# First block without GpSimd arithmetic: lower halves and three projection products moved to VectorE

## The chip, the cores and the metric

The program runs on one core of a Trainium2 chip, in one launch. The metric is the device time of one execution in microseconds (us), as the median of several runs. The engines of the core are TensorE (PE in the profile, with PEld for its weight loads), VectorE (DVE), ScalarE (ACT), GpSimd (POOL), and SyncE (SP), which here issues nearly all transfers. Each engine takes its own instructions in a fixed order and waits in that order for data of the others.

## The reference, cut to what matters

A sequence of 256 rows of 1024 numbers goes through a first block (an mLSTM group and a differential attention side by side, then a mixture of 32 experts) and through two layers of a second block, which this change does not touch. All arithmetic is float32. The part in question is the head of the first block:

```
h = rmsnorm(x, norm1_g)                    # 256 x 1024
proj = h @ w_in                            # 1024 x 3072, six parts of 512 columns
c, vm, z, qd, kd, vd = split(proj, 6)
y_m = mlstm_group(c, vm, z, ...)           # conv, gates, 4 heads, sigmoid(z) * h
y_d = diff_attention(qd, kd, vd, ...)      # 4 heads, each two softmaxes
x = x + concat(y_m, y_d) @ w_out
x = x + hier_moe(rmsnorm(x, norm2_g), ...) # router, 32 experts of 1024 x 512
```

## The kernel before, in words

A float32 product is made of three products of reduced-precision operands. Every operand is split into an upper half, which ScalarE writes by a cast (`whi` for weights, line 169; `xTh` for the input, line 388), and a lower half, which is the operand minus its upper half (`wlo`, line 173; `xTl`, line 389). TensorE then adds hi times hi, hi times lo and lo times hi into one PSUM tile.

The six parts of the projection run one after another, in the order c, vm, qd, kd, z, vd. The first five are `dense_T` (line 218): the result stands transposed, 4 x 128 columns by 256 rows, in two PSUM tiles `ps[0]` and `ps[1]`. Each takes eight blocks of 128 of the 1024 input columns, two blocks (one `split`, 128 x 1024 numbers) at a time, with 24 matmuls of 128x256 per split and 96 per part. There are four buffers for each kind of half, so a split waits until TensorE is done with the split four before it.

The input is not divided by the rows' norm before the products. The norm's factor `rn` (one number per row) is worked out by VectorE beside the first part (lines 395, 262 to 277, 397), spread over all partitions by two small TensorE products (line 425) into `R` (line 426), and every part's result is multiplied by `R` on its way out of PSUM: `cpad` (431), `vT` (436), `qd` (443 and 444), `kd` (457 and 458), `zs` (604 and 605).

GpSimd takes a share of this. It subtracts the lower halves of two of the four splits of part c and of all four of part vm (`pool=` in lines 420 and 433), the lower halves of the second half of the input (`NP = (1,)`, line 389), and the products with `R` for qd, kd and z, for which ScalarE first copies the PSUM tile to SBUF:

```
nc.scalar.copy(qd[:, 2 * c:2 * c + 2, :], ps[c])
nc.gpsimd.tensor_mul(qd[:, 2 * c:2 * c + 2, :], qd[:, 2 * c:2 * c + 2, :], R)
```

For a split whose lower half comes from GpSimd, `dense_T` puts the matmuls on `wlo` behind all matmuls on `whi` of that split (the `order.sort` of line 231).

The order of each engine's instructions is not the order of the code: a scheduler places them from their dependencies and priorities. `high_priority` pulls a piece ahead (the splits, and all of the mLSTM group under `early()`), and `issue_after` holds one back: the products of line 425 are tied behind the 81st matmul of part c (`r_behind = 80`). The mLSTM group (conv `cy`, `cth`, `ca`; gates `gt` to `um`; decay matrices `W` and `WS`; `HN`; `ym`) and the four attention heads (line 647 to 665) are thus placed among the matmuls of the parts qd to vd. Weights are loaded 1 MB at a time into four buffers, by SP; the experts' weights follow in the same queue (line 940) into rings that use memory the first block gives up.

The names in the rows: `raw` a loaded weight, `nh` the input times the norm's weight, `um` and `uT` the gates and their transpose, `BM` the table of relative biases (loaded by line 450 from `bigd`, which GpSimd's queue writes from `tb`), `mx` and `tp` small PSUM tiles, `acc` the large ones, `idle` a dummy operand.

Of the kernel before, what the change touches and what calls it, by code (L numbers as in the profile page):

```python
# [92 lines left out]
class K:  # L93
# [121 lines left out]
                    self.mm3(ps[t][:, :n], xh[:, kx + k, ts], xl[:, kx + k, ts], hi[:, k % 2, :n], lo[:, k % 2, :n],  # L215
                             first and k == 0, last and k == nk - 1)

    def dense_T(self, xT, kx, raw, nk, ps, hold={}, pool=()):

        xh, xl = xT
        mm = self.nc.tensor.matmul
        for k in range(0, nk, 2):
            with ExitStack() as es:
                for ins in hold.get(k, ()):
                    es.enter_context(self.tc.issue_after(ins.ins))
                hi, lo = self.split(raw, k, 2, 512, k in pool)
            order = [(j, c, i) for j in range(2) for c in range(4) for i in range(3)]
            if k in pool:  # L230
                order.sort(key=lambda z: z[2] == 2)
            for j, c, i in order:
                w, x = ((hi, xh), (hi, xl), (lo, xh))[i]
                first = k + j == 0 and i == 0
                ins = mm(ps[c // 2][:, c % 2, :], w[:, j, c * P:(c + 1) * P], x[:, kx + k + j, :],  # L235
                         start=first and c % 2 == 0, stop=k + j == nk - 1 and i == 2, skip_group_check=True)
                self.mms.append(ins)
                if first and c % 2 == 0:
                    head = ins
                elif first:  # L240
                    self.tc.add_manual_dep(ins.ins, head.ins.name, mybir.DependencyInfo(
                        mybir.DependencyClass.NoSync, mybir.DependencyReason.DATA))
# [76 lines left out]
    def first_mixers(self, x, outer):  # L319
        nc, tc, A = self.nc, self.tc, self.A  # L320
        with ExitStack() as es:
# [5 lines left out]
            hT = self.hT = self.xT_tile(8, self.yp, "xT")  # L327
            half = lambda: pz.tile([P, 512], F32, name="nh", bufs=4)
            w_in = A["w_in"][0]
            wc = []  # L330
            for n in range(2):
                raw = self.wp.tile([P, 4, 512], F32, name="raw")
# [15 lines left out]
            wv = self.load(w_in[:, 512:1024], D, 512)  # L348
# [20 lines left out]
            hold = {}  # L369
            with early():  # L370

                ps = self.tp.tile([P, 4, P], F32, name="tp")
# [3 lines left out]
            for n in range(2):  # L376
                for t in range(NT):
                  with tc.high_priority(offset=3000 if n == 0 else 900):
                    ps = self.tp.tile([P, 4, P], F32, name="tp")
                    for i in range(4):  # L380
                        cs = slice(n * 512 + i * P, n * 512 + (i + 1) * P)
                        nc.tensor.transpose(ps[:, i, :], x[:, t, cs], self.ident)
                    h = half().rearrange("p (i q) -> p i q", i=4)
                    with tc.issue_after(hold[2][1].ins) if n else ExitStack():
                        nc.vector.tensor_tensor(h, ps, gc[:, 4 * n:4 * n + 4].unsqueeze(2).to_broadcast([P, 4, P]),
                                                op=ALU.mult)
                    hi, lo = (z[:, 4 * n:4 * n + 4, t * P:(t + 1) * P] for z in hT)
                    hold[4 * n + 2 * t] = (nc.scalar.copy(hi, h),
                                           (nc.gpsimd if n in self.NP else nc.vector).tensor_sub(lo, h, hi))  # L389
            hold = {2: hold[2], 4: hold[6], 6: hold[6]}  # L390
            ss = pz.tile([P, NT, 2], F32, name="nss")
            for t in range(NT):
# [24 lines left out]

            ps = self.accT()
            self.mms = []
            self.dense_T(hT, 0, wc, 8, ps, hold, (0, 2))  # L420
            R = p.tile([P, S], F32, name="R")
            pr = self.tp.tile([P, 4, P], F32, name="tp")
            with early(), tc.issue_after(self.mms[self.r_behind].ins):
# [3 lines left out]
            R = R.unsqueeze(1).to_broadcast([P, 2, S])  # L427
# [2 lines left out]
            for c in range(2):  # L430
                nc.vector.tensor_mul(cpad[:, 2 * c:2 * c + 2, 3:], ps[c], R)
            ps = self.accT()
            self.dense_T(hT, 0, wv, 8, ps, pool=(0, 2, 4, 6))
            vT = pz.tile([P, 4, S], F32, name="vT")
            for c in range(2):
                nc.vector.tensor_mul(vT[:, 2 * c:2 * c + 2, :], ps[c], R)
# [2 lines left out]
            ps = self.accT()  # L439
            self.dense_T(hT, 0, self.load(w_in[:, 1536:2048], D, 512), 8, ps)  # L440
            qd = p.tile([P, 4, S], F32, name="qd", tag="qd", bufs=1)
            for c in range(2):
                nc.scalar.copy(qd[:, 2 * c:2 * c + 2, :], ps[c])
                nc.gpsimd.tensor_mul(qd[:, 2 * c:2 * c + 2, :], qd[:, 2 * c:2 * c + 2, :], R)
            self.mms = []
            ps = self.accT()
            self.dense_T(hT, 0, self.load(w_in[:, 2048:2560], D, 512), 8, ps)
# [6 lines left out]
                                 self.c("zc")[:, P:].unsqueeze(1).to_broadcast([P, 4, P]))  # L454
            kd = p.tile([P, 4, S], F32, name="kd", tag="kd", bufs=1)
            for c in range(2):
                nc.scalar.copy(kd[:, 2 * c:2 * c + 2, :], ps[c])
                nc.gpsimd.tensor_mul(kd[:, 2 * c:2 * c + 2, :], kd[:, 2 * c:2 * c + 2, :], R)
            with early():
                ca = pz.tile([P, 4, S], F32, name="ca")  # L460
                for c in range(4):
# [83 lines left out]
                for t in range(NT):  # L545
# [3 lines left out]
                    for h2 in range(2):  # L549
                        pn = self.mx.tile([P, 2, P + 1], F32, name="mx")  # L550
                        num.append(pn)
                        for j in range(2):
                            h = 2 * h2 + j
# [46 lines left out]
            ps = self.accT()  # L600
            self.dense_T(hT, 0, self.load(w_in[:, 1024:1536], D, 512), 8, ps)
            zs = p.tile([P, 4, S], F32, name="zs")
            for c in range(2):
                nc.scalar.copy(zs[:, 2 * c:2 * c + 2, :], ps[c])
                nc.gpsimd.tensor_mul(zs[:, 2 * c:2 * c + 2, :], zs[:, 2 * c:2 * c + 2, :], R)
                nc.scalar.activation(zs[:, 2 * c:2 * c + 2, :], zs[:, 2 * c:2 * c + 2, :], AF.Tanh, scale=0.5)
            nc.vector.tensor_scalar(zs, zs, 0.5, 0.5, op0=ALU.mult, op1=ALU.add)
            vd = p.tile([P, NT, 512], F32, name="vd")
# [3 lines left out]
            ps = self.accs(2, side)  # L612
# [704 lines left out]
            (nc.vector.tensor_copy if c % 2 else nc.scalar.copy)(dst[c], ps[c])  # L1317

    ahead = 1000
    NP = (1,)  # L1320

    EH = (0, 0, 0, 2)
    r_behind = 80
# [8 lines left out]
    hold = ()  # L1332
# [768 lines left out]
```

## Time and profile before

| what | value |
|---|---|
| median of 3 runs | 1774.81 us (1773.97 to 1777.96) |
| the profiled execution's own time | 1774.42 us |
| its span in the profile | 1772.70 us, mean TensorE clock 0.988 of full |
| TensorE busy | 1717.6 us (97%) |
| VectorE busy | 976.3 us (55%) |
| ScalarE busy | 740.3 us (42%) |
| GpSimd busy | 99.3 us (6%) |

Busy time of TensorE is modelled: a matmul counts until its result is out, and matmuls overlap, so 97% does not say that the engine did all it could. A row of the timeline gives start, duration, engine, line, operation, output and inputs; in brackets stands the idle time of the engine just before, and what ended it. Times run from the span's start. The first block up to the experts takes the first 172 us or so; the experts follow until about 610 us.

### The profile page before, as it was taken

Reading aid. Unit: us, or ns where it says so; the run is one execution under the profiler, and the core shown is the slowest. Engines: PE = TensorE matmul, PEld = TensorE weight load, DVE = VectorE, ACT = ScalarE, POOL = GpSimd, SP = SyncE. Lnnn points to the kernel's source line nnn. Section 1 sums busy time; section 2 is a strip of 40 time slices with the busy share of each in tenths; the row PEclk is TensorE's granted clock in tenths of the full one; section 3 lists DMA queues with packets and bytes.
Section 4 is the critical chain, followed back from the end, with each engine's and each line's share of the span. In section 5 each row is a group of like instructions: output and inputs, shape, how many; then the busy total and the mean of one; then the engine's idle time right before and its main releaser. Section 6 shows DMA issues by size and latency. Waiting matters only on the chain. (4 is left out here: it accounts for less than half of the span.)

```text
span 1772.7 us, 27358 instructions
## 1 busy us (share of the span) xinstructions
PE 1717.6 (97%) x11007; PEld 1315.3 (74%) x11007; DVE 976.3 (55%) x1868; ACT 740.3 (42%) x1260; POOL 99.3 (6%) x153
## 2 busy tenths in 40 slices
PE   7999999999999999999989999999999998999998
PEld 6876443444334379799878999987889987999997
DVE  6686122222222277764675765557766467575555
ACT  3463111111011146564644454444566464455443
POOL 4010000000000020000011000002000002000000
PEclk8999999999999999999999999999999999999999
DMA  8457999999999974256445755554335644455552
GB/s 266 147 210 298 413 420 420 420 418 420 420 420 419 413 235 136 69 179 199 148 144 160 237 188 187 187 176 157 112 93 179 202 143 131 167 173 186 188 190 83
DMA packets 153465, 414.51 MB, mean 234 GB/s; under 512 B 13347, under 2 KB 42868, under 8 KB 128632
## 3 DMA queue, kind: packets, MB, share of 16 engines
q1 hardware_dynamic: 152408, 410.49, 64.5%
q0 software_dynamic: 784, 2.18, 0.4%
q8 instruction: 87, 1.43, 0.3%
q14 instruction: 42, 0.34, 0.1%
q10 hardware_dynamic: 144, 0.07, 0.0%
HBM read 411.63 MB, written 2.12 MB: 233 GB/s over the span
## 5 line engine op out<-in xcount | busy, mean ns | idle before, releaser
L173 DVE TENSOR_TENSOR wlo<-raw,whi 128x1024 fp32r<-128x1024 f32 (+3 forms) x376 | 445.7, 1187 | 297.9 <-ACT whi L169 297.3
L169 ACT CAST whi<-raw 128x1024 fp32r<-128x1024 f32 (+4 forms) x384 | 385.2, 1005 | 396.3 <-PE acc L235 161.2
L235 PE MATMUL acc<-xTh,whi 128*128 128x256 f32 x992 | 286.5, 290 | 0.0
L235 PE MATMUL acc<-xTl,whi 128*128 128x256 f32 x992 | 284.2, 288 | 1.0 <-DVE xTl L389 1.0
L235 PE MATMUL acc<-xTh,wlo 128*128 128x256 f32 x992 | 279.6, 289 | 0.0
L1084 PE MATMUL acc<-raw,XT 128*64 128x512 f32 x1024 | 243.0, 603 | 3.8 <-DMA raw<-in_w_eg 2.7
L235 PEld LDWEIGHTS acc<-xTl,whi 128*128 128x128 f32 x992 | 192.6, 194 | 5.3 <-issue 3.5
L235 PEld LDWEIGHTS acc<-xTh,whi 128*128 128x128 f32 x992 | 192.6, 194 | 3.4 <-issue 2.4
L235 PEld LDWEIGHTS acc<-xTh,wlo 128*128 128x128 f32 x992 | 188.7, 193 | 5.6 <-issue 5.0
L1084 PEld LDWEIGHTS acc<-raw,XT 128*64 128x64 f32 x1024 | 74.6, 137 | 129.1 <-issue 115.4
L181 PE MATMUL acc<-wlo,xTh 128*128 128x512 f32 (+4 forms) x368 | 129.4, 352 | 1.7 <-DVE wlo L173 1.7
L182 PE MATMUL acc<-whi,xTl 128*128 128x512 f32 (+4 forms) x368 | 129.0, 351 | 0.2
L180 PE MATMUL acc<-whi,xTh 128*128 128x512 f32 (+4 forms) x368 | 128.5, 349 | 0.0
L1107 PE MATMUL acc<-raw,hidT 128*64 128x512 f32 x512 | 119.2, 597 | 4.4 <-DMA raw<-in_w_ed 4.2
L180 PE MATMUL acc<-whi,ffh 128*128 128x512 f32 x256 | 100.9, 394 | 0.0
L182 PE MATMUL acc<-whi,ffl 128*128 128x512 f32 x256 | 100.4, 392 | 0.0
L181 PE MATMUL acc<-wlo,ffh 128*128 128x512 f32 x256 | 100.4, 392 | 0.0
L1107 PEld LDWEIGHTS acc<-raw,hidT 128*64 128x64 f32 x512 | 35.6, 137 | 71.7 <-issue 61.4
L1049 DVE SCALAR_TENSOR_TENSOR yl<-acc,gs,yh 128x512 fp32r<-128x512 f32 x32 | 24.0, 751 | 107.0 <-ACT yh L1048 107.0
L1048 ACT ACTIVATE yh<-acc,gs 128x512 fp32r<-128x512 f32 x32 | 22.0, 687 | 140.0 <-PE acc L1107 140.0
L181 PEld LDWEIGHTS acc<-wlo,xTh 128*128 128x128 f32 x368 | 69.2, 188 | 10.6 <-DVE wlo L173 2.8
L182 PEld LDWEIGHTS acc<-whi,xTl 128*128 128x128 f32 x368 | 69.2, 188 | 7.8 <-DVE xTl L302 1.5
(690 smaller groups left out, 3061.4 us busy)
## 6 DMA issues: line engine op xcount, KB each, us to landing
raw<-in_w_in SPq DMA_DIRECT2D x70, 1024.0 KB, 5.1
raw<-in_w_eg SPq DMA_DIRECT2D x64, 1024.0 KB, 19.9
raw<-in_w_eu SPq DMA_DIRECT2D x64, 1024.0 KB, 19.9
raw<-in_w_ed SPq DMA_DIRECT2D x64, 1024.0 KB, 19.9
raw<-in_w_ff SPq DMA_DIRECT2D x64, 1024.0 KB, 5.2
raw<-in_w_out SPq DMA_DIRECT2D x12, 1024.0 KB
raw<-in_w_branch SPq DMA_DIRECT2D x12, 1024.0 KB, 5.4
raw<-in_w_in SPq DMA_DIRECT2D x8, 792.0 KB, 4.7
```

The lines of the kernel that those rows point to most:

```text
L169: nc.scalar.copy(hi[:, :nk, :n], src)
L173: ins = (nc.gpsimd if pool else nc.vector).tensor_sub(lo[:, :nk, :n], src, hi[:, :nk, :n])
L180: mm(ps, ahi, bhi, start=start, stop=False)
L181: mm(ps, ahi, blo, start=False, stop=False)
L182: self.mm_ins = mm(ps, alo, bhi, start=False, stop=stop)
L235: ins = mm(ps[c // 2][:, c % 2, :], w[:, j, c * P:(c + 1) * P], x[:, kx + k + j, :], start=first and c % 2 == 0, stop=k + j == nk - 1 and ...
L1048: nc.scalar.activation(yh[:rows], py[n][:rows], AF.Copy, scale=gs)
L1049: nc.vector.scalar_tensor_tensor(yl[:rows], py[n][:rows], gs, yh[:rows].bitcast(F32), op0=ALU.mult, op1=ALU.subtract)
L1084: nc.tensor.matmul(ps[64 * z:64 * z + 64], XT[:, k, 64 * (o + z):64 * (o + z + 1)], ww[z][k], start=k == 0, stop=k == 7)
L1107: nc.tensor.matmul(py[n][64 * z:64 * z + 64], hT[:, k, 64 * z:64 * z + 64], ww[z][k][:, n * 512:(n + 1) * 512], start=k == 0, stop=k == 3)
```

## The change

All lower halves of `dense_T` and of the input are subtracted by VectorE, the special order of matmuls for GpSimd's splits goes, and the products with `R` for qd, kd and z are done by VectorE straight from PSUM, without ScalarE's copy.

```diff
-    def dense_T(self, xT, kx, raw, nk, ps, hold={}, pool=()):
+    def dense_T(self, xT, kx, raw, nk, ps, hold={}):
...
-                hi, lo = self.split(raw, k, 2, 512, k in pool)
-            order = [(j, c, i) for j in range(2) for c in range(4) for i in range(3)]
-            if k in pool:
-                order.sort(key=lambda z: z[2] == 2)
-            for j, c, i in order:
+                hi, lo = self.split(raw, k, 2, 512)
+            for j, c, i in [(j, c, i) for j in range(2) for c in range(4) for i in range(3)]:
...
-                                           (nc.gpsimd if n in self.NP else nc.vector).tensor_sub(lo, h, hi))
+                                           nc.vector.tensor_sub(lo, h, hi))
...
-            self.dense_T(hT, 0, wc, 8, ps, hold, (0, 2))
+            self.dense_T(hT, 0, wc, 8, ps, hold)
...
-            self.dense_T(hT, 0, wv, 8, ps, pool=(0, 2, 4, 6))
+            self.dense_T(hT, 0, wv, 8, ps)
...
-                nc.scalar.copy(qd[:, 2 * c:2 * c + 2, :], ps[c])
-                nc.gpsimd.tensor_mul(qd[:, 2 * c:2 * c + 2, :], qd[:, 2 * c:2 * c + 2, :], R)
+                nc.vector.tensor_mul(qd[:, 2 * c:2 * c + 2, :], ps[c], R)
...
-                nc.scalar.copy(kd[:, 2 * c:2 * c + 2, :], ps[c])
-                nc.gpsimd.tensor_mul(kd[:, 2 * c:2 * c + 2, :], kd[:, 2 * c:2 * c + 2, :], R)
+                nc.vector.tensor_mul(kd[:, 2 * c:2 * c + 2, :], ps[c], R)
...
-                nc.scalar.copy(zs[:, 2 * c:2 * c + 2, :], ps[c])
-                nc.gpsimd.tensor_mul(zs[:, 2 * c:2 * c + 2, :], zs[:, 2 * c:2 * c + 2, :], R)
+                nc.vector.tensor_mul(zs[:, 2 * c:2 * c + 2, :], ps[c], R)
```

The scheduler places the whole first block anew. Line numbers of the changed kernel are smaller by 3 in the first lines, by 5 or so behind the products. VectorE from the first input tile to the norm, before:

```order
L385 TENSOR_TENSOR nh<-tp,gc 128x512 x2
L389 TENSOR_TENSOR xTl<-nh,xTh 128x4x128 x2
L385 TENSOR_TENSOR nh<-tp,gc 128x512 x2
L173 TENSOR_TENSOR wlo<-raw,whi 128x1024 x2
L401 COPY vec<-tp 128x32
L598 TENSOR_SCALAR dg<-vec 128x1
L395 TENSOR_TENSOR nss<-nss 128x2
L262 TENSOR_SCALAR rs_v<-nss,eps 128x2
```

VectorE at the same place in the changed kernel:

```order
L382 TENSOR_TENSOR nh<-tp,gc 128x512 x2
L173 TENSOR_TENSOR wlo<-raw,whi 128x1024
L386 TENSOR_TENSOR xTl<-nh,xTh 128x4x128 x2
L173 TENSOR_TENSOR wlo<-raw,whi 128x1024
L382 TENSOR_TENSOR nh<-tp,gc 128x512 x2
L386 TENSOR_TENSOR xTl<-nh,xTh 128x4x128 x2
L173 TENSOR_TENSOR wlo<-raw,whi 128x1024 x2
L398 COPY vec<-tp 128x32
L593 TENSOR_SCALAR dg<-vec 128x1
L392 TENSOR_TENSOR nss<-nss 128x2
L259 TENSOR_SCALAR rs_v<-nss,eps 128x2
```

Four instructions more stand ahead of the norm (two `wlo`, two `xTl`); two further `wlo` stand inside the norm's chain and two behind it, ahead of `R`. TensorE around the two products that spread the norm, before (`acc_229` and `acc_230` belong to part c, `acc_352` and `acc_353` to part vm):

```order
L235 MATMUL acc_230<-xTh,whi 128x256
L235 MATMUL acc_230<-xTl,whi 128x256
L235 MATMUL acc_230<-xTh,wlo 128x256
L425 MATMUL tp<-const,rn 128x128 x2
L235 MATMUL acc_230<-xTh,whi 128x256
L235 MATMUL acc_230<-xTl,whi 128x256
L235 MATMUL acc_230<-xTh,wlo 128x256
```

TensorE there in the changed kernel:

```order
L232 MATMUL acc_230<-xTh,wlo 128x256
L232 MATMUL acc_352<-xTh,whi 128x256
L232 MATMUL acc_352<-xTl,whi 128x256
L232 MATMUL acc_352<-xTh,wlo 128x256
L232 MATMUL acc_352<-xTh,whi 128x256
L422 MATMUL tp<-const,rn 128x128 x2
L232 MATMUL acc_352<-xTl,whi 128x256
L232 MATMUL acc_352<-xTh,wlo 128x256
```

The products on `rn` stood behind 81 matmuls of the projections and stand behind 100 now, four into part vm. VectorE around the gates, where qd ends, before:

```order
L516 TENSOR_SCALAR NM<-Mx 4x256
L453 TENSOR_TENSOR BM<-BM,const 128x4x128
L517 TENSOR_TENSOR um<-NM,bb 4x256
L173 TENSOR_TENSOR wlo<-raw,whi 128x1024
L523 COPY uT<-mx 128x72
L536 SCALAR_TENSOR_TENSOR W<-mx,uT,const_132 128x256
```

VectorE at that place in the changed kernel (`acc_487` and `acc_488` hold part qd):

```order
L511 TENSOR_SCALAR NM<-Mx 4x256
L440 TENSOR_TENSOR qd<-acc_487,R 128x512
L512 TENSOR_TENSOR um<-NM,bb 4x256
L440 TENSOR_TENSOR qd<-acc_488,R 128x512
L173 TENSOR_TENSOR wlo<-raw,whi 128x1024
L449 TENSOR_TENSOR BM<-BM,const 128x4x128
L518 COPY uT<-mx 128x72
L531 SCALAR_TENSOR_TENSOR W<-mx,uT,const_132 128x256
```

The two products for qd come in, one ahead of `um` and one behind it, and `BM` moves from ahead of `um` to behind the `wlo`. On TensorE four matmuls of part kd now stand between the first `NM` product (line 531) and the first product on `qk` (line 533). The products for kd stand in VectorE's queue inside the second norm of the mLSTM group, those for z inside its third; the attention heads are interleaved with that group in another order. In SP's queue the only move is the fourth load of `w_out`, which stood behind the first two expert loads and now stands ahead of them. GpSimd keeps its memsets and its two transfers for the bias table. Behind the first block the order is unchanged on every engine, but for a GpSimd set-up instruction that stands at that engine's first arithmetic.

## Rows read from the trace of the kernel before

**Rows 1.** Stretches: busy time of each engine, TensorE clock, DMA share, GB/s.

```profile
50.00:89.00 39.00, 37.13 (x262) 32.24 (x262) 29.00 (x58) 17.76 (x25) 3.30 (x2) 0.91 0.45 145
89.00:127.00 38.00, 35.17 (x224) 28.98 (x224) 33.54 (x114) 25.71 (x64) 5.73 (x4) 1.00 0.50 184
...
172.60:177.60 5.00, 4.95 (x24) 2.13 (x26) 0.76 (x2) 0.10 (x1) 0.00 (x0) 1.00 0.20 39
177.60:600.00 422.40, 415.21 (x1964) 172.26 (x1962) 104.31 (x190) 58.87 (x110) 0.00 (x0) 0.99 1.01 419
```

**Rows 2.** TensorE's waits, 0 to 200 us: total, times, longest.

```profile
PE tp L425 <- DVE rn L397: 4.5, 1, 4.5
...
PE mx L478 <- DVE tb L409: 1.5, 1, 1.5
...
PE mx L533 <- DVE uT L523: 1.4, 1, 1.4
...
PE mx L675 <- ACT vd L615: 1.1, 1, 1.1
PE acc L235 <- DVE xTl L389: 1.0, 1, 1.0
...
PE acc L641 <- POOL kd L458: 0.7, 1, 0.7
```

**Rows 3.** Timeline of GpSimd, from 8 us: start, duration, instruction, wait before.

```profile
8.27 2.36 POOL L173 TENSOR_TENSOR wlo<-raw,whi 128x1024 fp32r<-128x1024 f32 x1 [5.44 <-ACT whi L169]
...
18.40 7.25 POOL L173 TENSOR_TENSOR wlo<-raw,whi 128x1024 fp32r<-128x1024 f32 x3 [0.32 <-ACT whi L169]
...
65.66 3.30 POOL L444 TENSOR_TENSOR qd<-qd,R 128x512 f32<-128x512 f32 x2 [18.81 <-ACT qd L443]
```

**Rows 4.** Timeline of VectorE in the same stretches.

```profile
8.74 3.05 DVE L389 TENSOR_TENSOR xTl<-nh,xTh 128x512 fp32r<-128x512 f32 x2 [1.32 <-ACT xTh L388]
...
19.35 1.52 DVE L395 TENSOR_TENSOR nss<-nss 128x2 f32<-128x2 f32 x1
20.90 2.34 DVE L262 TENSOR_SCALAR rs_v<-nss,eps 128x2 f32<-128x2 f32 x1
...
23.48 2.19 DVE L267 TENSOR_SCALAR rs_i<-rs_i 128x2 int32<-128x2 int32 x1
...
65.72 0.67 DVE L453 TENSOR_TENSOR BM<-BM,const 128x512 f32<-128x512 f32 x1
66.43 1.40 DVE L517 TENSOR_TENSOR um<-NM,bb 4x256 f32<-4x256 f32 x1
67.86 2.18 DVE L173 TENSOR_TENSOR wlo<-raw,whi 128x1024 fp32r<-128x1024 f32 x1
```

**Rows 5.** VectorE by line and shape, 0 to 130 us: busy, mean ns.

```profile
L431 DVE TENSOR_TENSOR cpad<-acc,R 128x512 f32<-128x512 f32 x2 | 1.4, 692 | 2.1 <-PE acc L235 2.1
...
L276 DVE SCALAR_TENSOR_TENSOR rs_q<-rs_q,rs_v 128x2 f32<-128x2 f32 x3 | 0.5, 161 | 0.1
```

**Rows 6.** The page's costliest group: busy, mean ns.

```profile
L173 DVE TENSOR_TENSOR wlo<-raw,whi 128x1024 fp32r<-128x1024 f32 (+3 forms) x376 | 445.7, 1187 | 297.9 <-ACT whi L169 297.3
```

**Rows 7.** TensorE at the wait for the norm.

```profile
27.78 0.55 PE L425 MATMUL tp<-const,rn 128*128 128x128 f32 x1 [4.46 <-DVE rn L397]
```

**Rows 8.** Stretches at full and at half clock, columns as in rows 1.

```profile
18.00:20.00 2.00, 2.00 (x19) 2.00 (x18) 1.50 (x4) 1.37 (x2) 1.68 (x2) 1.00 1.06 413
28.40:32.40 4.00, 4.00 (x21) 4.00 (x21) 1.31 (x3) 0.41 (x1) 0.00 (x0) 0.50 0.27 32
70.40:76.80 6.40, 6.40 (x21) 4.94 (x21) 3.32 (x7) 2.02 (x4) 0.00 (x0) 0.50 0.50 164
```

**Rows 9.** SP's queue: start, duration, issue.

```profile
31.54 4.38 SPq L159 DMA_DIRECT2D raw<-in_w_in  x4
53.48 3.67 SPq L450 DMA_DIRECT2D BM<-bigd  x8
```

**Rows 10.** DMA issues of the bias table: KB each, median us to landing.

```profile
BM<-bigd SPq DMA_DIRECT2D x8, 64.0 KB, 2.2
```

More of the change, by code (lines that the diff above doesn't have):

```diff
@@ L1319 @@
     ahead = 1000
-    NP = (1,)
     EH = (0, 0, 0, 2)
```

## The prediction

> **What bounds the kernel now.** I read the table of stretches first. From 177.6 us to 600 us the experts take their weights as fast as the DMA engines move them: share 1.01, 419 GB/s [rows 1]. So there TensorE, though modelled as busy, is fed by the transfers. Just ahead of it, from 172.6 to 177.6 us, the DMA share is only 0.20 at 39 GB/s [rows 1]: the rings are full, and transfers go on only when the first experts free their buffers. The time at which the first block ends therefore starts everything after it, and since the order behind the block does not change, a microsecond gained in the first block should be a microsecond of the whole. That is the first step of the forecast.
>
> Second, the waits of TensorE up to 200 us: one of 4.5 us for `rn`, and then 1.5 (`tb`), 1.4 (`uT`), 1.1 (`vd`), 1.0 (`xTl`) and 0.7 (`kd`) [rows 2]. [...]
>
> Fourth, why `rn` and `uT` are late. GpSimd's three subtractions run from 18.40 for 7.25 us, to 25.65 [rows 3], about 2.4 us each. Beside them VectorE's tiny operations on 128x2 numbers take 1.52, 2.34 and 2.19 us and end at 20.87, 23.24 and 25.67 [rows 4], at the ends of GpSimd's instructions. An operation of that size takes 161 ns when nothing runs beside it [rows 5]. So VectorE stands still while GpSimd subtracts. The same shows beside GpSimd's two products (65.66 us, 3.30 us [rows 3]): `um` of 4x256 takes 1.40 us and the `wlo` behind it 2.18 us [rows 4] against a mean of 1.187 [rows 6].
>
> **The change part by part.** The sum is made against the profiled execution's own 1774.42 us (1.72 of it outside the span), which is 0.39 under the median of 1774.81.
>
> *VectorE's load.* It gains six `wlo`: 6 x 1.187 = 7.1 us [rows 6]. It gains two `xTl`: the pair at 8.74 took 3.05 beside GpSimd [rows 4]; alone I take the 0.69 us of a 128x512 operation [rows 5] for each, 1.4 together. And it gains six products with `R` from PSUM, of the same shape and source as `cpad`: 6 x 0.692 = 4.2 us [rows 5]. Together +12.7 us. It loses the stretches. Of the rows shown: 3.05 - 1.4, 1.52 + 2.34 + 2.19 - 3 x 0.16, 1.40 - 0.4 (my estimate for 4x256, from `BM`'s 0.67 for 512 numbers per partition [rows 4]) and 2.18 - 1.19, in sum 9.2 us, and these are only part of the places where GpSimd works. So VectorE's load hardly rises, and it falls where TensorE waits for it. GpSimd's arithmetic and six copies of ScalarE go; nobody waits for what they leave free.
>
> *Term A, up to 50 us.* In the new order TensorE meets the norm's products behind 100 matmuls instead of 81. It came there at 27.78 - 4.46 = 23.3 us [rows 7]; 19 matmuls at 19 in 2.0 us [rows 8] add 2.0, and the wait of 1.0 for `xTl` ahead of it [rows 2] falls away: 24.3. On VectorE the chain from 19.35 us to the products at 27.78 [rows 4, 7] lasted 8.4 us, 5.6 of it stretch; alone 2.8, and with the two `wlo` put inside it 5.2. What comes ahead of the chain is two `wlo` and two `xTl` more (3.8) and a stretch of 1.7 less at 8.74; at least 1.3 of the difference fits into VectorE's idle time there (1.32 in one row alone [rows 4]), so the chain starts about where it did and `rn` is ready near 24.6. Left of the wait: 0.3. If the cover failed and all 2.1 came on top, the wait would be 2.4. With the wait gone the clock should stay up: the 21 matmuls from 28.4 to 32.4 took 4.0 us and take 21 x 2.0 / 19 = 2.2 at full clock [rows 8], 1.8 back. The waits for `xTl` (1.0) and `tb` (1.5), both VectorE's work beside GpSimd [rows 2], go with the stretch. A = 4.5 - 0.3 + 1.8 + 1.0 + 1.5 = 8.5 us less. Bounds: 2.1 if only the difference at the norm is gained and the clock falls all the same (4.5 - 2.4), 9.0 at most.
>
> *Term B, 50 to 89 us.* VectorE is busy 29.00 of 39 us here [rows 1]. On the way to `uT` the stretch of `um` (1.0) and of the `wlo` behind it (1.0) go, `BM` (0.67) moves from ahead of `um` to behind it and stays on the way, and the two products for qd (1.4) come in. VectorE is thus 0.6 us earlier, and four matmuls of part kd now stand on TensorE ahead of the product that waits, 4 x 2.0 / 19 = 0.4 [rows 8]. Of the 1.4 I leave 0.6, and count 0.8. The half clock from 70.4 to 76.8 us gives back up to 3.2 of its 6.4 us [rows 8] if it does not fall. I take all 3.2, since the idle time ahead is less than half of what it was and has matmuls of 128x256 inside it; B = 4.0 less. Bounds: 4.6 less (the wait gone as well), or 0.5 more if `uT` gets later by half the added products.
>
> GpSimd's queue also writes the bias table that `BM` needs. SP's loads of it are issued from 53.48 for 3.67 us [rows 9] and land 2.2 us later [rows 10], at 59.35, and VectorE takes it at 65.72 [rows 4], 6.4 us of slack. The table starts from VectorE's `tb`, so most of its transfer moves along when VectorE gets earlier; were it to stay at its old time while VectorE's `BM` came 8.5 us earlier, less the 3.0 us of `um`, qd and `wlo` put ahead of it (0.4 + 1.4 + 1.2), 0.9 us of slack would be left.
>
> *Term C, 89 to 127 us.* VectorE is busy 33.54 of 38 us [rows 1]. It gains four products, 2.8 us [rows 5], and loses the stretch beside GpSimd's 5.73 busy us [rows 1], at most 5.7 and by the share of the 65.66 place (2.0 of 3.30) some 3. TensorE's waits for `vd` and `kd`, 1.1 + 0.7 [rows 2], are for ScalarE and GpSimd, whose part in them shrinks. I count 1.0 less. Bounds: 1.8 less, or 2.8 more if all four products stand on the path. *The fourth load of w_out*, put ahead of two expert loads, delays those by 1 MB, some 2.5 us at 419 GB/s [rows 1]; the nearly idle DMA of 172.6 to 177.6 hides it.
>
> Sum: 8.5 + 4.0 + 1.0 = 13.5 less, 1760.9 us for an execution like the profiled one, and with its 0.39 a median of 1761.3 us.
>
> **The rivals.** *The clock falls anyway and VectorE binds behind kd.* For it: 0.6 us of the wait for `uT` is still there, and VectorE is already busy 88% from 89 to 127 [rows 1]. Then B brings nothing and C turns from 1.0 less to 2.5 more: 1761.3 + 4.0 + 3.5 = 1768.8. Against it: the load hardly rises.
>
> *The bias table comes late.* The row above shows slack of 6.4 us shrinking, to 0.9 at the worst. If the table lands 2 us behind VectorE's want of it, VectorE stands ahead of `uT`, term B goes (4.0) and 2.0 come on top: 1767.3. No row shows that transfer delayed. [...]
>
> *No change.* If the experts' start hung on a transfer of fixed time, the block's gain would be given back and the time stay at 1774.8. The share of 0.20 from 172.6 to 177.6 [rows 1] speaks against it.
>
> *Slower.* The PSUM tiles of kd and z were freed by ScalarE (busy 25.71 of 38), and are now freed by VectorE (33.54 of 38) [rows 1], which takes them only when its queue of gates and heads comes to them. If TensorE waited at each of these four tiles as long as it did for the norm, 4.5 us [rows 2], that is +18 and 1779.3. It decides from 3.4 us a tile on (13.5 / 4). Against it: TensorE had only 1.8 us of waits there, and VectorE has 4.5 us of room.
>
> **How the numbers follow.** The forecast 0.62, with its own range of 1757 to 1766 (term A's clock, B's clock, C's bounds); the fallen clock 0.19; the late table 0.04; no change 0.06; slower 0.09. The 8-in-10 range goes from 1756 to 1770.5 and takes in the first two rivals. A measurement of this kernel tells about 0.2% (3.5 us) from no change. Faster by more: 0.62 + 0.19 + 0.04 = 0.85, and 0.01 for a weaker form of "no change"; within: 0.05; slower: 0.09.
>
> **What would show it.** No operation of 128x2 on VectorE over 0.3 us up to 30 us; no wait over 1 us at the norm's products, and TensorE's clock at 1.00 from 28 to 34 us; part vm ending 8 to 9 us earlier; `uT` waited for by under 0.8 us and no stretch at 0.50 behind it; from 80 us on the same work 12 to 13 us earlier, and no wait for VectorE over 1 us at kd, z and the heads; the first expert's start and the end of the span earlier by the same amount. The forecast is wrong if TensorE stands at a PSUM tile that VectorE has not yet multiplied, if a half clock appears at another place, or if the first block's gain is not found at 600 us.

## The result: 1757.3 us, and the profile after

The changed kernel took 1757.3 us (median of 5 runs, 1755.61 to 1757.93), the kernel before, in the same job, 1777.96. The ratio is 0.9885, 95% interval 0.987 to 0.99. In the profiled executions the span fell from 1772.70 to 1756.1 us, by 16.6. The forecast was 1761.3: faster by somewhat more than forecast. How much the change saves is known less well than that it saves: between medians taken together it is 20.7 us here, 19.7 and 15.9 on two other chips (1776.04 and 1756.3, 1775.23 and 1759.36), and the profiled execution of before (1774.42) is one of its faster ones.

Of TensorE's waits up to 200 us that [rows 2] shows, one is left; the list (total, times, longest) now begins with the load of the input; waits of the router follow, which stood there before as well:

```profile
PE tp L379 <- DMA x<-in_x: 3.4, 1, 3.4
...
PE acc L232 <- DVE xTl L386: 0.2, 1, 0.2
```

VectorE beside the norm and beside `uT`, the counterpart of [rows 4]:

```profile
15.23 1.29 DVE L386 TENSOR_TENSOR xTl<-nh,xTh 128x512 fp32r<-128x512 f32 x2
...
19.57 0.16 DVE L392 TENSOR_TENSOR nss<-nss 128x2 f32<-128x2 f32 x1
19.77 0.23 DVE L259 TENSOR_SCALAR rs_v<-nss,eps 128x2 f32<-128x2 f32 x1
...
20.24 0.17 DVE L264 TENSOR_SCALAR rs_i<-rs_i 128x2 int32<-128x2 int32 x1
...
24.36 0.17 DVE L394 COPY rn<-rs_i 128x2 f32<-128x2 f32 x1
...
57.94 0.42 DVE L512 TENSOR_TENSOR um<-NM,bb 4x256 f32<-4x256 f32 x1
58.38 0.69 DVE L440 TENSOR_TENSOR qd<-acc,R 128x512 f32<-128x512 f32 x1
58.99 1.22 DVE L173 TENSOR_TENSOR wlo<-raw,whi 128x1024 fp32r<-128x1024 f32 x1
60.13 0.68 DVE L449 TENSOR_TENSOR BM<-BM,const 128x512 f32<-128x512 f32 x1
```

The 128x2 operations that took 1.52, 2.34 and 2.19 us take 0.16, 0.23 and 0.17; the pair of `xTl` 1.29 instead of 3.05; `um` 0.42 instead of 1.40. TensorE meets its two former waits without one (no bracket behind the row):

```profile
25.78 0.60 PE L422 MATMUL tp<-const,rn 128*128 128x128 f32 x4
...
61.01 0.70 PE L528 MATMUL mx<-qk 128*128 128x256 f32 x2
```

The stretches of [rows 1, 8] (columns as there), the last two shifted by the 16.2 us that the experts now start earlier:

```profile
28.40:32.40 4.00, 4.00 (x36) 4.00 (x35) 4.00 (x11) 0.40 (x2) 0.00 (x0) 1.00 0.49 50
50.00:89.00 39.00, 38.98 (x277) 33.74 (x276) 32.46 (x107) 17.72 (x39) 0.00 (x0) 1.00 0.53 176
70.40:76.80 6.40, 6.40 (x51) 6.01 (x50) 5.96 (x23) 1.68 (x2) 0.00 (x0) 1.00 0.50 166
89.00:127.00 38.00, 37.88 (x220) 32.36 (x218) 31.53 (x83) 25.68 (x58) 0.00 (x0) 1.00 0.66 250
156.40:161.40 5.00, 5.00 (x24) 2.05 (x26) 0.76 (x2) 0.01 (x1) 0.00 (x0) 1.00 0.15 29
161.40:600.00 438.60, 431.14 (x2031) 178.09 (x2027) 107.13 (x195) 60.97 (x114) 0.00 (x0) 0.99 1.01 419
```

Both half clocks of [rows 8] are gone, TensorE is nearly without a gap from 50 to 127 us (38.98 of 39.00 and 37.88 of 38.00), and the experts run at 419 GB/s as before, from an earlier start.

To place the gain I cut the first block at six events of the timeline: the first projection product, the end of the last `vT`, the first product on `uT` (line 528), the first product with `V` and `WS`, the first with `vd` and `aT`, and the end of the last sum into `x` after `w_out`. The lengths in us, with those of all experiments:

| kernel | to `vT` | to `uT` | to `V,WS` | to `vd,aT` | to `x` | sum |
|---|---|---|---|---|---|---|
| before | 40.94 | 19.21 | 11.61 | 43.42 | 31.53 | 146.7 |
| after | 31.18 | 18.51 | 8.75 | 39.17 | 31.55 | 129.2 |
| after_again | 31.55 | 18.50 | 8.75 | 39.17 | 31.54 | 129.5 |
| after_third | 31.35 | 18.51 | 8.76 | 39.16 | 31.53 | 129.3 |
| gp_reads_norm | 38.36 | 18.50 | 8.77 | 39.21 | 31.55 | 136.4 |
| gp_writes_norm | 32.99 | 18.50 | 8.76 | 39.22 | 31.51 | 131.0 |
| gp_reads_ut | 30.93 | 19.98 | 11.78 | 39.20 | 31.56 | 133.5 |
| products_only | 43.67 | 18.48 | 8.75 | 39.20 | 31.53 | 141.6 |
| halves_only | 30.99 | 19.27 | 10.07 | 43.44 | 31.53 | 135.3 |
| kd_z_back | 31.43 | 18.52 | 8.76 | 41.66 | 31.46 | 131.8 |
| copy_kept | 30.30 | 18.52 | 8.40 | 39.90 | 35.57 | 132.7 |

after_again and after_third are the changed kernel once more, on the chips of other experiments. Its three executions agree within 0.02 us in all stages but the first, which spreads by 0.37. Over all ten executions here that have the changed kernel's order up to `vT` and nothing added, the first stage takes 30.1 to 31.6 us. Whole times scatter by several us, mostly behind the first block (the three spans are 1756.1, 1758.0 and 1754.9 us, their sums here 129.2 to 129.5), so the stages tell more than the medians.

A stage does not always hold the same work. The third and the fourth, before and then after:

```profile
70.24:81.85 11.61, 11.61 (x51) 9.25 (x51) 5.87 (x12) 3.23 (x6) 0.00 (x0) 0.71 0.28 90
81.85:125.27 43.42, 40.59 (x270) 34.24 (x268) 38.91 (x138) 28.06 (x63) 5.73 (x4) 1.00 0.46 163
```

```profile
61.01:69.76 8.75, 8.75 (x53) 7.16 (x54) 5.78 (x13) 3.77 (x7) 0.00 (x0) 1.00 0.74 274
69.76:108.93 39.17, 39.17 (x264) 33.73 (x262) 36.74 (x141) 24.54 (x59) 0.00 (x0) 1.00 0.46 162
```

Six matmuls of 128x256 that stood in the fourth stage now stand in the second (four) and the third (two). TensorE's busy time in the fourth falls by 1.4 us for that, and its idle time from 2.8 us to nothing.

### The profile page after: what moved, and what is told of

It reads as the page before. It is cut to its first block, busy times and chain, and to the rows that moved or that the text cites. A ratio compares the mean times of both kernels' runs of the same rounds, so it can differ in the third digit from the quotient of the medians.

```text
span 1756.1 us, 27356 instructions
## 1 busy us (share of the span) xinstructions
PE 1710.9 (97%) x11007; PEld 1310.5 (75%) x11007; DVE 971.2 (55%) x1882; ACT 737.0 (42%) x1254; POOL 72.2 (4%) x139
## 5 line engine op out<-in xcount | busy, mean ns | idle before, releaser
L232 PE MATMUL acc<-xTh,wlo 128*128 128x256 f32 x992 | 285.0, 287 | 0.0
```

## Experiments

The theory: GpSimd instructions that read SBUF hold VectorE up; the gain is the sum of what that cost in each stage, with the clock that falls behind TensorE's waits. The rival: the gain comes from other queues and another order of matmuls, and the long VectorE rows cost nothing.

**GpSimd's reading brought back, for nobody.** The order of the other engines stays word for word.

```diff
+            dum = pz.tile([P, 4, S], F32, name="dum", tag="ca", bufs=1)
+            with tc.high_priority(offset=3000), tc.issue_after(hold[6][1].ins):
+                for _ in range(3):
+                    nc.gpsimd.tensor_sub(dum, hT[1][:, 4:8, :], hT[0][:, 4:8, :])
```

> The changed kernel, and three more subtractions of 128x1024 on GpSimd, of the input's second lower and upper half, into a scratch tile that nobody reads. They can start when VectorE's last xTl is written, about 16.6 us, and last some 7 us, beside the norm. The order of all other engines is the same. Theory (GpSimd reading SBUF holds VectorE up): VectorE's wlo at 16.8 and the 128x2 operations of the norm end at the ends of GpSimd's instructions, rn comes 5 to 7 us later, TensorE waits 4 to 6 us for it and its clock falls for some 4 us behind; 1757.3 + 6 to 9 = 1763 to 1766. Rival (the gain came only from whose queue the lower halves and products stand in, and from the order of the matmuls): nobody waits for the added work, the time stays at 1757.

Measured: 1765.43 us (ratio to before 0.9945, 0.9925 to 0.9966). GpSimd and then VectorE in that kernel:

```profile
15.29 9.09 POOL L391 TENSOR_TENSOR dum<-xTl,xTh 128x1024 f32<-128x1024 f32 x3 [12.46 <-DVE xTl L386]
```

```profile
15.46 6.66 DVE L173 TENSOR_TENSOR wlo<-raw,whi 128x1024 fp32r<-128x1024 f32 x2 [0.26 <-ACT whi L169]
...
22.32 2.08 DVE L396 TENSOR_TENSOR nss<-nss 128x2 f32<-128x2 f32 x1
...
29.22 0.17 DVE L398 COPY rn<-rs_i 128x2 f32<-128x2 f32 x1
```

TensorE's waits that it brings back, and its clock (the third figure from the end) from 30 to 34 us:

```profile
PE acc L232 <- DVE wlo L173: 3.4, 3, 2.1
...
PE tp L426 <- DVE rn L398: 1.6, 1, 1.6
```

```profile
30.00:34.00 4.00, 4.00 (x23) 4.00 (x23) 3.96 (x8) 0.00 (x0) 0.00 (x0) 0.57 0.26 24
```

Work that nobody reads makes the first stage 7.0 us longer (38.36 against 31.36, the mean of the three) and no other. The 4 to 6 us of waiting that I expected at `rn` are there, but 3.4 of the 5.0 stand at `wlo`. Where the two meet, GpSimd's subtraction takes 3.0 us instead of 2.4 (9.09 for three) and VectorE's 3.3 instead of 1.2. `nss`, which reads two tensors as `wlo` does, takes 2.08 us instead of 0.16. The rival falls for term A.

**Writing instead of reading.**

```diff
+                nc.gpsimd.tensor_sub(dum[:, 0, 0:8], hT[1][:, 7, 248:256], hT[0][:, 7, 248:256])
+                for _ in range(7):
+                    nc.gpsimd.memset(dum, 0.0)
```

> The changed kernel, and seven memsets of 128x1024 on GpSimd at the same place (behind one tiny subtraction that holds them until 16.6 us), some 7 us of writing to SBUF without reading. Theory: only reading holds VectorE up; no VectorE operation is longer than without it and the time stays at 1757. Rival (any GpSimd instruction holds VectorE up): rn comes 5 to 7 us later and the time is 1763 to 1766 as with the three subtractions.

Measured: 1760.11 us (0.9922, 0.9894 to 0.995); first stage 1.6 us longer than the mean of the three, and TensorE waits 1.6 us for `rn`. Neither theory holds. VectorE in that kernel:

```profile
15.93 2.36 DVE L173 TENSOR_TENSOR wlo<-raw,whi 128x1024 fp32r<-128x1024 f32 x2 [0.26 <-ACT whi L169]
...
18.73 0.16 DVE L397 TENSOR_TENSOR nss<-nss 128x2 f32<-128x2 f32 x1 [0.15 <-ACT nh L396]
18.92 1.46 DVE L259 TENSOR_SCALAR rs_v<-nss,eps 128x2 f32<-128x2 f32 x1
20.41 0.97 DVE L263 TENSOR_SCALAR rs_i<-rs_v 128x2 int32<-128x2 int32 x1
21.42 0.98 DVE L264 TENSOR_SCALAR rs_i<-rs_i 128x2 int32<-128x2 int32 x1
```

The operations on two tensors are as short as without the memsets (2.36, 0.16); the three of one tensor and a scalar take about a memset each (GpSimd's rows: three in 2.98 us from 16.02, four in 3.99 us from 19.41). So in these rows writing holds up the 128x2 operations of one tensor and a scalar (the one of 128x1 at 18.42 us took 0.15), and reading those of both kinds (2.08 for `nss` in gp_reads_norm, 2.34 and 2.19 for the TENSOR_SCALAR of [rows 4]).

**The same at `uT`.** GpSimd's two products for qd are doubled for nobody.

```diff
                 nc.vector.tensor_mul(qd[:, 2 * c:2 * c + 2, :], ps[c], R)
+                if c == 0:
+                    zs = p.tile([P, 4, S], F32, name="zs")
+                    for _ in range(2):
+                        nc.gpsimd.tensor_mul(zs[:, 0:2, :], qd[:, 0:2, :], R)
...
-            zs = p.tile([P, 4, S], F32, name="zs")
```

> The changed kernel, and two more GpSimd products of 128x512 that read the first half of qd and R as soon as VectorE has written it (57.9 us) and write into the still unused tile of z, as GpSimd's products for qd did before. The order of all other engines is the same. Theory: the wlo behind qd takes about 2 us instead of 1.2, and uT comes 1.5 to 2.5 us later, TensorE waits 1.5 to 2.5 us; if this alone brings the clock down as before, another 2 to 3: 1757.3 + 1.5 to 5 = 1759 to 1762. Rival (term B came from the new order, not from the missing GpSimd work): 1757.

Measured: 1762.58 us (0.9926, 0.9902 to 0.9951), just above the range expected, against 1756.3 of the changed kernel on the same chip. GpSimd and VectorE there, the wait, and TensorE's clock behind it:

```profile
57.58 3.73 POOL L444 TENSOR_TENSOR zs<-qd,R 128x512 f32<-128x512 f32 x2 [12.05 <-DVE qd L440]
```

```profile
57.97 0.69 DVE L440 TENSOR_TENSOR qd<-acc,R 128x512 f32<-128x512 f32 x1
58.58 1.60 DVE L173 TENSOR_TENSOR wlo<-raw,whi 128x1024 fp32r<-128x1024 f32 x1
60.10 1.76 DVE L453 TENSOR_TENSOR BM<-BM,const 128x512 f32<-128x512 f32 x1
```

```profile
PE mx L532 <- DVE uT L522: 1.5, 1, 1.5
```

```profile
64.00:68.00 4.00, 4.00 (x17) 3.35 (x17) 1.89 (x4) 0.52 (x1) 0.00 (x0) 0.50 0.95 349
```

This brings back term B and no more: 1.5 us until `uT` and 3.0 us at half clock behind it, 4.5 in all, with the order of the changed kernel. The product that reads PSUM (57.97) is not held up beside GpSimd (0.69 us), the ones from SBUF are (1.60 and 1.76, in the changed kernel 1.22 and 0.68).

**One half of the change alone.** The kernel before with the products on VectorE (the three places of the diff, two instructions each), and the changed kernel with those six put back:

> The kernel before with the six products with R moved to VectorE; the lower halves of parts c and vm and of the input's second half stay on GpSimd. Theory (the saving is a sum by place): term A, measured as 8.6 us at the end of part vm, is lost, the other 8 us stay: 1757 + 8.6 = 1766, with the wait for rn of 4 to 5 us and the half clock behind it back. Rival (the products carry the whole, the early gain is taken up by a later wait): 1757 to 1759.

> The changed kernel with the six products with R put back on ScalarE's copy and GpSimd; all lower halves on VectorE. Theory (sum by place): term A is kept, so part vm ends near 41 us; what 50 to 127 us gave, 8 us, is lost: 1757 + 8 = 1765, with the wait for uT and half clock behind it. Rival (the early lower halves carry the whole): 1757 to 1759.

Measured: products_only 1769.91 us (0.9959, 0.9945 to 0.9972), halves_only 1766.36 us (0.9943, 0.9928 to 0.9958). In products_only stages two to four are those of the changed kernel to 0.04 us, and the first is 2.7 us longer than before, which puts the time 3.9 above the 1766 expected: VectorE's `xTl` meets two subtractions of GpSimd back to back, which start at 9.52 and 12.20 us there and at 8.27 and 11.64 in the profile of before, and TensorE waits 3.7 us for it instead of 1.0. Up to `vT` the order is that of the kernel before, so the first stage of before is itself known from two executions that differ by 2.7 us.

```profile
9.52 2.37 POOL L173 TENSOR_TENSOR wlo<-raw,whi 128x1024 fp32r<-128x1024 f32 x1 [6.70 <-ACT whi L169]
12.20 2.44 POOL L173 TENSOR_TENSOR wlo<-raw,whi 128x1024 fp32r<-128x1024 f32 x1 [0.31 <-ACT whi L169]
```

```profile
9.99 5.19 DVE L389 TENSOR_TENSOR xTl<-nh,xTh 128x512 fp32r<-128x512 f32 x2 [2.59 <-ACT xTh L388]
```

In halves_only the first stage is the short one (30.99) and the fourth the long one (43.44), with the waits of before:

```profile
PE mx L530 <- DVE uT L520: 1.4, 1, 1.4
...
PE mx L672 <- ACT vd L612: 1.1, 1, 1.1
...
PE acc L638 <- POOL kd L455: 0.7, 1, 0.7
...
PE mx L554 <- DVE HN L568: 0.5, 1, 0.5
PE tp L660 <- DVE pe L656: 0.4, 1, 0.4
```

So the lower halves make term A, and moving the products is enough for the whole of B and C (products_only). Neither half carries the whole, and both rivals fall. Putting the products back costs C in full but only 2.1 of B's 3.6 us: the wait for `uT` is that of before (1.4), but the mean clock of the stage behind it is 0.83 (10.07 us) instead of 0.71 (11.61 us).

**Only the products for kd and z put back.**

> The changed kernel with only the products for kd and z put back on ScalarE's copy and GpSimd; qd and all lower halves on VectorE. Theory: A and B stay, of what 89 to 127 us gave (4.2 us) most is lost: 1757 + 3 to 5 = 1760 to 1762, with waits for kd, vd and HN on TensorE. Rival (part C's saving was only the shifted order): 1757.

Measured: 1761.69 us (0.9914, 0.9887 to 0.9941). The fourth stage gives back 2.5 of its 4.25 us (41.66); B stays whole. TensorE waits 0.7 us for `kd`, as before, and 1.0 for `dsm`; the waits for `vd` and `HN` that I expected are not there. The remaining 1.8 come with qd's product on VectorE, though it stands ahead of this stage: with it the scheduler moves the six matmuls out of the stage (TensorE busy 39.74 us instead of 40.64 in halves_only), and places the heads in another order (idle 1.92 instead of 2.80).

**The copy kept, GpSimd out.** In all three places:

```diff
-                nc.vector.tensor_mul(qd[:, 2 * c:2 * c + 2, :], ps[c], R)
+                nc.scalar.copy(qd[:, 2 * c:2 * c + 2, :], ps[c])
+                nc.vector.tensor_mul(qd[:, 2 * c:2 * c + 2, :], qd[:, 2 * c:2 * c + 2, :], R)
```

> The changed kernel, but ScalarE copies qd, kd and z out of PSUM as before and VectorE multiplies in SBUF; GpSimd has no part in it. It tells whether the saving behind 50 us comes from GpSimd's absence or from the copy that is left out. Theory (GpSimd's absence): 1757 to 1759. Rival (the missing hand-over and ScalarE's missing work): most of the 8 us behind 50 us is lost, 1762 to 1765.

Measured: 1762.99 us (0.9917, 0.9886 to 0.9948): in the rival's range, but not where the rival put it. Stages two to four keep the gain but 0.4 us (8.40 and 39.90), and TensorE does not wait in them, so there GpSimd's absence is what counts. The fifth is 4.0 us longer: TensorE waits 2.3 us for `vd`, since the scheduler puts the products on `yqd` behind it, and the lower clock that follows takes the other 1.7:

```profile
PE mx L674 <- ACT vd L612: 2.3, 1, 2.3
```

```profile
112.00:116.00 4.00, 4.00 (x19) 3.72 (x19) 1.62 (x2) 1.70 (x9) 0.00 (x0) 0.57 1.02 422
```

This kernel's order differs from the changed kernel's, so what the copy itself costs is not shown.

**GpSimd's other arithmetic moved too.** Behind 600 us, in the second block:

```diff
-            nc.gpsimd.tensor_add(B[:, :, 0:P], B[:, :, 0:P], cm)
-            nc.gpsimd.tensor_add(B[:, :, S:], B[:, :, S:], cm)
+            nc.vector.tensor_add(B[:, :, 0:P], B[:, :, 0:P], cm)
+            nc.vector.tensor_add(B[:, :, S:], B[:, :, S:], cm)
...
-        g = self.nc.gpsimd
+        g = self.nc.vector
...
-                    (nc.gpsimd if i < 3 else nc.vector).tensor_add(m, m, t2)
+                    nc.vector.tensor_add(m, m, t2)
```

> The changed kernel, and the other GpSimd arithmetic that reads SBUF moved to VectorE too, all of it behind 600 us: the sums of the mixed branches (16 of 128x512), the two additions to fB (16 of 128x256) and the rotations of the second block (40 small ones). The same theory (GpSimd's reads hold VectorE up) with the condition that TensorE has to wait for VectorE there: its waits for VectorE behind 600 us add up to 19 us, of which 8.3 are for Pr and 5.1 for gO; the former do not stand beside these GpSimd instructions. So 0 to 3 less: 1754 to 1757.5. Rival (GpSimd's absence pays wherever it works): about 35 us of GpSimd's work gone, 10 less. Second rival (VectorE fuller than before delays TensorE): 3 more.

> The changed kernel itself on the same chip, to compare rest_too with: 1756 to 1758, 0.9885 of the kernel before.

Measured: 1745.08 us (0.9824, 0.9808 to 0.9841), the changed kernel on the same chip 1759.36 (0.9911, 0.9892 to 0.993). My expectation was wrong; the first rival (10 less) came nearer. The normalisation of `Pr` in the changed kernel (line, shape, count, busy, mean ns), and then in rest_too:

```profile
L1359 DVE TENSOR_SCALAR Pr<-Pr,smx 128x256 f32<-128x256 f32 x48 | 22.7, 473 | 0.0
L1359 DVE TENSOR_SCALAR Pr<-Pr,smx 128x128 f32<-128x128 f32 x48 | 16.5, 344 | 0.7
```

```profile
L1359 DVE TENSOR_SCALAR Pr<-Pr,smx 128x256 f32<-128x256 f32 x48 | 16.7, 347 | 0.0
L1359 DVE TENSOR_SCALAR Pr<-Pr,smx 128x128 f32<-128x128 f32 x48 | 13.6, 283 | 0.8
```

TensorE's waits behind 600 us in the changed kernel, and in rest_too, where that for `Pr` is not in the list any more:

```profile
PE tp L1365 <- DVE Pr L1359: 8.0, 8, 1.4
PE tp L1748 <- DVE gO L1746: 5.0, 6, 1.6
```

```profile
PE tp L1748 <- DVE gO L1746: 3.1, 4, 1.2
```

I had taken it that the rows of `Pr` do not stand beside GpSimd. They are longer by 126 and 61 ns in the mean, and TensorE waits for them. The spans differ by 11.2 us (1754.9 and 1743.7), 10.3 of it behind the last product of the experts (606.04 and 605.10); the two waits shown account for 9.9.

The last two runs split this and go on. mixed_only has only the last line of that diff; all_vector is rest_too with

```diff
-                ins = (nc.gpsimd if pool else nc.vector).tensor_sub(lo[:, :nk, :n], src, hi[:, :nk, :n])
+                ins = nc.vector.tensor_sub(lo[:, :nk, :n], src, hi[:, :nk, :n])
```

> The changed kernel with only the 16 sums of the mixed branches (128x512) moved from GpSimd to VectorE; the additions to fB and the rotations stay on GpSimd. rest_too took away TensorE's waits of 8.0 us for Pr and some 3 us for gO, sbl and wlo, and this tells which GpSimd work made them. If the sums do (they stand beside the normalisation of Pr and beside gO): 1757.3 - 8 to 11 = 1746 to 1750. If the additions to fB and the rotations do: 1755 to 1758.

> rest_too, and the last two lower halves on GpSimd (128x1024, near 1172 us, at the change from the first to the second layer) moved to VectorE as well, where they stand inside the chain of 128x1 operations of the norm. If GpSimd's reading costs there too: 1745.1 - 1 to 3 = 1742 to 1744. If the two wlo of 1.19 us in the chain cost as much as the stretch did, since TensorE waits 2.2 us for nh there: 1745 to 1747.5.

Measured: mixed_only 1751.7 us (0.9847, 0.9831 to 0.9864), all_vector 1742.86 us (0.9801, 0.9785 to 0.9817). In mixed_only the wait for `Pr` is 0.8 instead of 8.0 us, and that for `gO` stays at 5.1; so the sums of the mixed branches made the one, the additions to `fB` or the rotations some of the other, and the range expected, 1746 to 1750, ended 1.7 too low. In all_vector the `nh` between the layers, which stood beside the first of GpSimd's two last subtractions, is short again (first the changed kernel of after_third, then all_vector), and TensorE's wait for it falls from 2.2 to 0.6 us:

```profile
1177.08 3.49 DVE L1899 SCALAR_TENSOR_TENSOR nh<-x,rs_i,G 128x512 f32<-128x512 f32 x2
```

```profile
1170.87 1.42 DVE L1899 SCALAR_TENSOR_TENSOR nh<-x,rs_i,G 128x512 f32<-128x512 f32 x2
```

all_vector is the fastest: 2.0% under the kernel before, of which the change studied here brings 1.15. Its interval and that of rest_too overlap, so this last step is shown by the rows of `nh` and not by the time.

## Why the prediction was right, and where its sum was off

- *The end of the first block sets the rest.* Right. The experts start 16.3 us earlier (first product at 156.36 instead of 172.65) and the span is 16.6 shorter.
- *VectorE stands still while GpSimd subtracts.* Shown by gp_reads_norm, which brings long rows (6.66 us for two `wlo` instead of 2.36) and waits (5.0 us) back with the order of the other engines unchanged.
- *VectorE's load hardly rises.* Right: 971.2 us busy in the whole program after, 976.3 before, though it does 14 instructions more. From 89 to 127 us it is less busy than before (31.53 and 33.54 us, though other work stands in that stretch now).
- *Term A, 8.5 less.* 9.6 from the first projection product (40.94 and 31.36), and 8.5 on the span's clock, for the first product starts 1.2 us later in the profiled execution of after (11.32 and 10.09 us), where TensorE waits 3.4 us for the input and in that of before 2.4. The parts of the forecast's upper bound add up to 8.8 and not to 9.0, and the gain is above both. `rn` was forecast for 24.6 us and was ready at 24.53, which is in part luck: with the input as early as before, `rn` is ready at 23.31 (after_again). TensorE came at 25.78, in after_again at 24.95, both later than the 24.3 worked out, and did not wait at all. The clock stayed at 1.00 (24 to 34 us). The gain hangs on the one profile of before: against the 43.67 of products_only it would be 12.3.
- *Term B, 4.0 less.* 0.7 until `uT` and 2.9 in the stage behind it, 3.6, with six matmuls more in these two stages. Counted as TensorE's idle time (1.3) and what the lower clock cost (29% of 11.61 us, 3.4) it is 4.7. gp_reads_ut gave nearly the same price from the other side, with the same matmuls in each stage (1.5 and 3.0). That the clock falls behind such waits, on which 1.8 of A and the 3.2 here rest, shows in three kernels: 0.50 in [rows 8], 0.57 in gp_reads_norm, 0.50 in gp_reads_ut; in gp_writes_norm it stayed at 1.00 behind 1.6 us.
- *Term C, 1.0 less.* This is the term that was mis-sized: the stage from `V,WS` to `vd,aT` gave 4.25. I had counted part of two waits of 1.8 us that [rows 2] shows and set VectorE's four added products against the stretch. In fact halves_only has the whole list of before in this stage, 1.1 + 0.7 + 0.5 + 0.4 = 2.7 us, and the changed kernel none of it. [Rows 1] had it: TensorE idle for 38.00 - 35.17 = 2.8 us between 89 and 127. The other 1.4 us are work that moved: the six matmuls that now stand in B's stages. So C is 2.8 us of waiting, above the forecast's 1.0 and its bound of 1.8: waits that [rows 2] does not show, and the whole of those that it shows, went with GpSimd's products.
- *The rivals.* The clock did not fall elsewhere between the norm and 127 us (1.00 from 34 to 127); VectorE did not become the bound behind kd. The bias table was in time: in the changed kernel VectorE takes it at 60.13 us, its loads were all issued at 54.50 and land 2.3 us later, which leaves 3.3. So about half of the slack of 6.4 went. GpSimd's queue feeds the table by two transfers: the one of 1 MB took 5.0 us from issue to landing against 7.5 before, but the one of 8 KB ahead of it (from `tb`) took 5.5 against 1.9. It now runs beside the weights' loads (DMA share 1.03 from 39.2 to 44.8 us; 0.24 from 43.7 to 45.8 before), with VectorE about as busy as before (3.83 of 5.60 us, 1.30 of 2.10). The loads are thus the likelier cause, but no run tries them alone. Nor does a run show the 2.0 us of lateness in that rival's sum; 3.3 us of slack were measured in its place. The slower case needed 3.4 us of waiting at each of the four tiles of kd and z; there was none.

The sum was 13.5 by the forecast; by stages it is 17.4 (146.7 - 129.3, the mean of the three). In the profiled pair 1.2 of that is lost to the input, which landed later: the experts start 16.3 us earlier. Of the 3.9 us by which the sum fell short, 1.1 belong to A and, counted by TensorE's waits and clock, 0.7 to B and 1.8 to C; the range was wide enough for them. The mechanism was right at all three places; what was too small was the price, of C above all.

## What to carry to other kernels

Where GpSimd and VectorE both work from SBUF, look for VectorE rows that are far longer than others of their shape and end with a GpSimd row: there GpSimd's help can cost more than it takes over. Here 128x1024 took it 2.4 us against VectorE's 1.2, and beside it three of VectorE's 128x2 operations took 1.52 to 2.34 us instead of 0.16 to 0.23. Compare the mean of a shape beside GpSimd with its shortest, and do it everywhere, also where the wait on TensorE looks as if it had another cause (`Pr`). A short wait of TensorE with a lower clock behind it cost two to three times its length here (1.4 and 1.7 us in halves_only, 1.5 and 3.0 in gp_reads_ut), so price the two together.

## What the runs showed of the hardware beyond that

- In gp_writes_norm memsets of 128x1024 on GpSimd hold up VectorE's TENSOR_SCALAR on 128x2 (0.97 to 1.46 us instead of 0.17 to 0.23), but neither the one on 128x1 (0.15) nor its TENSOR_TENSOR on 128x2 (0.16) or 128x1024 (2.36 for two).
- In gp_reads_ut, beside GpSimd's products, a VectorE TENSOR_TENSOR of 128x512 with one input in PSUM keeps its 0.69 us, while those from SBUF (128x1024 and 128x512) take 1.60 and 1.76 instead of 1.22 and 0.68.
- Behind 1.5 us of waiting at `uT` the granted clock fell to 0.50 (64 to 68 us, gp_reads_ut), which cost 3.0 us more; behind 1.6 us at `rn` in gp_writes_norm it did not fall (1.00 from 26 to 34 us, and the stage grew by the wait alone). What makes the difference was not tried.
